# The 16 small products of y's u part in each RWKV unit queued behind the unit's last chain product (1 core, float32 decoder layer)

## The chip, the cores and the metric

The kernel runs on one core of a Trainium2 chip. Every time is a device time in microseconds (us) of that core. A version's time is the median of its runs; one further execution is recorded by the hardware profiler, and all rows and intervals in this text are from that execution. TensorE is called PE (its weight loads PEld), VectorE DVE, ScalarE ACT, GpSimd POOL, and SyncE, which issues most of the DMAs, SP.

## The reference

One decoder layer in float32, 1024 tokens by 1024 channels: a SwiGLU feed-forward (inner width 2816) with layer norm; a token mixer; layer norm; a second feed-forward with layer norm. The mixer projects the tokens through `w_in` and runs two branches side by side, an mLSTM (4 heads of 256, chunks of 128 tokens) and an RWKV-7 recurrence (16 heads of 64), multiplies each branch with its weights, gates them with sigmoids, adds them and multiplies with `w_out`. The RWKV recurrence is

```python
def step(st, xs):
    r_t, w_t, k_t, v_t, a_t, b_t = xs
    sa = jnp.einsum('bhvk,bhk->bhv', st, a_t)
    st = st * w_t[:, :, None, :] + sa[..., None] * b_t[:, :, None, :] + v_t[..., None] * k_t[:, :, None, :]
    return st, jnp.einsum('bhvk,bhk->bhv', st, r_t)
```

The change touches how the outputs y of that recurrence are put together. No arithmetic is added or removed.

## The kernel before

**Stages.** Phase A is the first feed-forward, B the `w_in` projections and the RWKV recurrence, C the mLSTM with the branch product of RWKV, D the rest of the mixer and the second feed-forward. The large products are made as three products of split operands (L128, L129, L130; moving tile 128x512 or 128x256, type float32r). Those of phase B that nothing nearby waits for are called fillers here: `fillers` traces them with the lowest priority, and the scheduler puts them wherever PE would have nothing else. Their result goes to a `psg` tile. The RWKV projections for the next head pair go to `psa` by the same three lines.

**RWKV units.** A unit `u` is one pair of heads (`p = u // 2`) and one half of the tokens (`hh = u % 2`), 8 chunks of 64 tokens. The 16 units are worked one after the other. `rwkv_half` prepares a unit, `rwkv_scores` makes its score tiles `SC` (L495), `rwkv_inverse` fills the V part of the tile `UV` (transposes L551, ACT copies L554, POOL memsets L555) and inverts the triangular parts (L573, L580). `rwkv_post` normalises y and stores it to `yrD`.

**The chain.** `rwkv_chain` is serial over the 8 chunks of a unit: L599 and L600 add up the right-hand side in `psc`, DVE copies it into `RW` (L601, a view of the tile `AR`), L603 multiplies it by the inverse into `psd`, DVE copies that product, called u, into the free half of chunk n's `UV` (L605), L609 makes the state update, POOL decays the old state (L612) and DVE adds the two (L614); then the next chunk's L600 needs the new state. L603 is the unit's last chain product for chunk 7.

**y's u part.** `rwkv_out` makes 16 products `SC` by u of 64x64x64 in float32 (L629) into one `psb` tile: the even chunks (e = 0) first, a DVE addition (L630), then the odd chunks, and a second addition. A float32 matmul is issued once in the program and stands as two passes in the trace, so the 16 are the 32 of the change's name. Each product needs only its own chunk's u.

**What sets the order.** Each engine works through its own queue in order. That queue is laid down when the program is built: a scheduler takes traced instructions by priority as they become ready in its own reckoning. Chain and `rwkv_out` are both traced at priority 3000, inverse at 2000, fillers lowest. `psb` and `UV` have two buffers each, used in turn.

Of the kernel before, what the change touches and what calls it, by code (L numbers as in the profile page):

```python
# [30 lines left out]
class Net:  # L31
# [551 lines left out]
    def rwkv_chain(self, o):  # L583
        nc = self.nc
        AR, SC, BN, UV, XT, PC = (o[k] for k in ("AR", "SC", "BN", "UV", "XT", "PC"))
        H = [slice(0, 64), slice(64, 128)]
        fl = lambda t: t.rearrange("p h v -> p (h v)")

        RW = AR.rearrange("p n (e c) -> p (n e) c", c=P)
        if o["hh"] == 0:  # L590
            for h in range(2):
                nc.gpsimd.memset(self.Sbuf[1][H[h], h], 0.0)
        S = self.Sbuf[1]
        for n in range(8):
            n2, e = n // 2, n % 2
            bs = H[1 - e]
            pc = self.ps("c", (P, 2, 64))
            for h in range(2):
                nc.tensor.matmul(pc[:, h], SC[:, e, n2, h], UV[:, n, H[h]], start=h == 0, stop=False)  # L599
            nc.tensor.matmul(fl(pc), AR[:, n2, e * P:(e + 1) * P], fl(S), start=False, stop=True)  # L600
            nc.vector.tensor_copy(RW[:, n], fl(pc))  # L601
            pu = self.ps("d", (P, 2, 64))
            nc.tensor.matmul(fl(pu), fl(XT[:, e, n2]), RW[:, n], start=True, stop=True)  # L603
            for h in range(2):
                nc.vector.tensor_copy(UV[bs, n, H[h]], pu[H[h], h])  # L605
            if o["hh"] == 1 and n == 7:
                break
            pS = self.ps("d", (P, 2, 64))
            nc.tensor.matmul(fl(pS), BN[:, n], UV[:, n], start=True, stop=True)  # L609
            S1 = self.Sbuf[n % 2]  # L610
            pcn = PC[:, n:n + 1]
            nc.gpsimd.tensor_scalar(S1, S, pcn, None, op0=ALU.mult)  # L612
            for h in range(2):
                nc.vector.scalar_tensor_tensor(S1[H[h], h], pS[H[h], h], pcn[H[h]], S1[H[h], h],  # L614
                                               op0=ALU.mult, op1=ALU.add)
            S = S1
# [412 lines left out]
def build(tc, ins, out):  # L1029
    with ExitStack() as ctx:  # L1030
        net = Net(ctx, tc, ins, out)
        nc = tc.nc
# [26 lines left out]
        with net.phase("B", VB=4):  # L1059
            net.rwkv_small(x1T)  # L1060
            with net.low():
                for f in net.fillers(x1T):
                    f()
            pr = net.rwkv_prep(x1T, 0)
            units = [net.rwkv_half(pr, 0)]
            net.mlstm_gates(x1T)
            units.append(net.rwkv_half(pr, 1))
            net.rwkv_scores(units[0])
            net.rwkv_inverse(units[0])
            net.rwkv_scores(units[1])  # L1070
            for u in range(16):
                if u % 2 == 0 and u < 14:
                    pr = net.rwkv_prep(x1T, u // 2 + 1)
                with net.high(3000):
                    net.rwkv_chain(units[u])
                    net.rwkv_out(units[u])
                if u % 2 and u < 14:
                    units.append(net.rwkv_half(pr, 1))
                if u < 15:
                    with net.high(2000):  # L1080
                        net.rwkv_inverse(units[u + 1])
                if u % 2 == 0 and u < 14:
                    units.append(net.rwkv_half(pr, 0))
                if u < 14:
                    with net.high(3000):
                        net.rwkv_scores(units[u + 2])
                net.rwkv_post(units[u])
# [83 lines left out]
```

## Time and profile before

| | us |
|---|---|
| median of 3 runs (3355.88 to 3357.31) | 3355.94 |
| the profiled execution | 3345.49 |
| its span, first to last instruction | 3343.8 |
| PE busy | 3183.2 (95%) |
| DVE busy | 1706.0 (51%) |
| ACT busy | 832.3 (25%) |
| POOL busy | 760.9 (23%) |

The profiled execution took 3345.49 us, 0.31% less than the median. Its span leaves 1.7 us outside. PE is busy in nearly every slice, so what a step costs is read best from the starts of matmuls that follow each other: the durations of neighbouring matmuls overlap.

### The profile page before, as it was taken

The page shows a single profiled execution, that of the slowest core. Times are in us where ns is not written, and L with a number is a line of the kernel's source. Part 1 is how long each engine was busy: PE and PEld are TensorE (multiplying, and loading weights), DVE is VectorE, ACT ScalarE, POOL GpSimd, SP SyncE. Part 2 cuts the span into 40 slices and gives each one's busy share as a digit, 9 for nine tenths or more (in the row PEclk, how much of TensorE's full clock was granted, in tenths as well). Part 3 has the DMA queues.
Part 4 walks back from the last instruction along what each step waited for, and adds up shares of the span by engine and source line. Part 5 has one row for each costly group of instructions (what it writes and reads, how often), then busy time and mean ns, then how long its engine had stood idle before and what let it go on. Part 6 is the DMA issues. An engine that isn't in the chain of part 4 may idle for free. (4 is left out here: it accounts for less than half of the span.)

```text
span 3343.8 us, 43277 instructions
## 1 busy us (share of the span) xinstructions
PE 3183.2 (95%) x16344; PEld 2585.9 (77%) x16344; DVE 1706.0 (51%) x4350; ACT 832.3 (25%) x1327; POOL 760.9 (23%) x755
## 2 busy tenths in 40 slices
PE   9999999998899999999999999999988999999997
PEld 7888888877677777887877777777776888888886
DVE  3323222264647676757667675576478322232227
ACT  3121112122312231313222221464333211111111
POOL 3222222222212222222222131200003222222212
PEclk9999999999989999999999999999999999999999
DMA  4111111113222232222232333554562111111111
GB/s 152 51 44 44 51 51 51 45 45 88 59 57 65 66 85 64 73 58 70 68 75 58 79 85 82 184 183 140 182 222 92 57 51 46 50 44 57 45 32 51
DMA packets 386903, 259.33 MB, mean 78 GB/s; under 512 B 102365, under 2 KB 342151, under 8 KB 386695
## 3 DMA queue, kind: packets, MB, share of 16 engines
q1 hardware_dynamic: 379783, 243.98, 25.1%
q0 software_dynamic: 4608, 8.39, 0.9%
q10 hardware_dynamic: 2304, 4.20, 0.3%
q8 instruction: 129, 2.11, 0.3%
q14 instruction: 79, 0.65, 0.1%
HBM read 203.02 MB, written 53.48 MB: 77 GB/s over the span
## 5 line engine op out<-in xcount | busy, mean ns | idle before, releaser
L206 DVE SCALAR_TENSOR_TENSOR v<-v,psb 128x512 f32<-128x512 f32 (+1 forms) x92 | 61.1, 665 | 737.3 <-PE psb L130 726.6
L232 DVE SCALAR_TENSOR_TENSOR u<-u,psc 128x512 f32<-128x512 f32 x416 | 282.8, 685 | 209.6 <-PE psc L130 205.6
L128 PE MATMUL psc<-u,u 128*128 128x512 f32 x832 | 331.1, 398 | 15.5 <-DVE u L232 7.0
L128 PE MATMUL psg<-xT,w 128*128 128x512 f32 (+1 forms) x856 | 329.9, 385 | 8.6 <-DVE v L962 6.0
L129 PE MATMUL psg<-xT,w 128*128 128x512 f32 (+1 forms) x856 | 330.3, 386 | 0.6 <-DVE xT L112 0.6
L129 PE MATMUL psc<-u,u 128*128 128x512 f32 x832 | 326.7, 393 | 3.4 <-DVE u L112 3.4
L130 PE MATMUL psg<-xT,w 128*128 128x512 f32 (+1 forms) x856 | 328.9, 384 | 0.0
L130 PE MATMUL psc<-u,u 128*128 128x512 f32 x832 | 326.7, 393 | 2.1 <-DVE u L112 2.0
L128 PE MATMUL psg<-xT,wf 128*128 128x512 f32 x776 | 316.9, 408 | 4.4 <-DVE f L686 2.1
L112 POOL TENSOR_TENSOR wf<-rawf,wf 128x512 fp32r<-128x512 f32 x186 | 255.4, 1393 | 280.3 <-ACT wf L108 243.0
L129 PE MATMUL psg<-xT,wf 128*128 128x512 f32 x776 | 317.2, 409 | 0.0
L130 PE MATMUL psg<-xT,wf 128*128 128x512 f32 x776 | 317.1, 409 | 0.0
L112 POOL TENSOR_TENSOR w<-raw,w 128x512 fp32r<-128x512 f32 x139 | 176.9, 1292 | 581.2 <-ACT w L108 513.9
L130 PE MATMUL psb<-xT,wf 128*128 128x512 f32 (+1 forms) x744 | 284.7, 383 | 0.0
L128 PE MATMUL psb<-xT,wf 128*128 128x512 f32 (+1 forms) x744 | 284.1, 382 | 0.5 <-ACT wf L108 0.5
L129 PE MATMUL psb<-xT,wf 128*128 128x512 f32 (+1 forms) x744 | 284.3, 382 | 0.0
L112 POOL TENSOR_TENSOR u<-u,u 128x1024 fp32r<-128x1024 f32 x44 | 105.5, 2398 | 603.3 <-ACT u L108 425.0
L108 ACT CAST w<-raw 128x512 fp32r<-128x512 f32 x163 | 96.8, 616 | 477.7 <-PE psg L129 176.0
L128 PEld LDWEIGHTS psc<-u,u 128*128 128x128 f32 x832 | 157.5, 189 | 63.6 <-DVE u L232 21.3
L108 ACT CAST wf<-rawf 128x512 fp32r<-128x512 f32 x210 | 123.4, 619 | 332.1 <-PE psg L129 154.8
L128 PEld LDWEIGHTS psg<-xT,w 128*128 128x128 f32 x856 | 161.4, 189 | 42.9 <-DVE v L962 6.8
L129 PEld LDWEIGHTS psg<-xT,w 128*128 128x128 f32 x856 | 161.4, 189 | 32.8 <-DVE xT L112 2.1
(325 smaller groups left out, 6108.4 us busy)
## 6 DMA issues: line engine op xcount, KB each, us to landing
rawf<-in_w_in_dram SPq DMA_DIRECT2D x98, 256.0 KB
raw<-in_ffn_w_gate_dram SPq DMA_DIRECT2D x88, 256.0 KB
rawf<-in_ffn_w_up_dram SPq DMA_DIRECT2D x88, 256.0 KB
u<-in_ffn_w_down_dram SPq DMA_DIRECT2D x44, 512.0 KB
raw<-in_w_in_dram SPq DMA_DIRECT2D x50, 256.0 KB
qkD<-f SPq DMA_DIRECT2D x32, 256.0 KB
v<-wadD POOLq DMA_DIRECT2D x32, 256.0 KB, 4.0
gD<-f SPq DMA_DIRECT2D x32, 256.0 KB
```

The source lines that it names most:

```text
L108: nc.scalar.copy(hi, src)
L112: eng.tensor_tensor(lo, src, hi.bitcast(F32), op=ALU.subtract)
L128: mm(out, a[0], b[0], start=first, stop=False)
L129: mm(out, a[0], b[1], start=False, stop=False)
L130: mm(out, a[1], b[0], start=False, stop=last)
L206: nc.vector.scalar_tensor_tensor(hf, sg, 0.5, pu, op0=ALU.mult, op1=ALU.mult)
L232: nc.vector.scalar_tensor_tensor(yd, yd, ALPHA if first else 1.0, po, op0=ALU.mult, op1=ALU.add)
```

## The change

The last L603 of a unit is kept (`o["last"]`, overwritten in each chunk), and `rwkv_out` is traced inside `tc.issue_after` of it. That adds an edge of order, and no wait for completion, from each PE instruction of `rwkv_out` to that product: on PE no L629 of a unit may stand ahead of the unit's last L603. Other engines get no edge.

```diff
@@ rwkv_chain
             pu = self.ps("d", (P, 2, 64))
-            nc.tensor.matmul(fl(pu), fl(XT[:, e, n2]), RW[:, n], start=True, stop=True)
+            o["last"] = nc.tensor.matmul(fl(pu), fl(XT[:, e, n2]), RW[:, n], start=True, stop=True)
@@ build
                     net.rwkv_chain(units[u])
-                    net.rwkv_out(units[u])
+                    with tc.issue_after(units[u]["last"].ins):
+                        net.rwkv_out(units[u])
```

The scheduler lays all later queues anew, so the order differs from unit 0 until the end of phase C. Counted over the whole of PE's queue, the 256 L629 stand in 99 rows of the order before (a row is a run of like instructions with nothing between) and in 46 after. In units with odd number they stood as 8 and 8 already; in the even ones and in unit 15 they stood in up to 11 places. The other small products stand in nearly the same number of rows: L599 128 before and 132 after, L495 41 and 42, L551 17 and 18, L660 23 and 24, L437 21 and 20, all others unchanged.

PE's queue in the middle of unit 2's chain before: L603 with one chunk's u product, L609 with its state update, L629 with y's products of unit 2, L130, L128 and L129 with fillers, L599 already of unit 3.

```order
L603 MATMUL psd_11281<-AR_10303,XT_735_5121 128x128
L599 MATMUL psc_11623<-UV_11323,SC_10804 128x64 x2
L130 MATMUL psg_6022<-xT_4577,wf_6013 128x512
L629 MATMUL psb_11304<-UV_10749,SC_10378 64x64
L128 MATMUL psg_6022<-xT_4577,wf_6012 128x512
L609 MATMUL psd_11285<-UV_10749,BN_10488 128x128
L629 MATMUL psb_11304<-UV_10749,SC_10378 64x64
L129 MATMUL psg_6022<-xT_4578,wf_6012 128x512
```

Here two of y's products stand alone, one between fillers and one behind the state update. The same unit's end after, from its last L603 (L551 are the V transposes of unit 3, into whose `UV` the L599 of unit 3 look):

```order
L603 MATMUL psd_11295<-AR_10303,XT_735_5121 128x128
L629 MATMUL psb_11304<-UV_10749,SC_10378 64x64 x7
L609 MATMUL psd_11299<-UV_10749,BN_10488 128x128
L629 MATMUL psb_11304<-UV_10749,SC_10378 64x64
L551 MATMUL psb_11324<-ident,vv_10111 128x128 x4
L130 MATMUL psg_6098<-xT_4577,wf_6089 128x512
L128 MATMUL psg_6126<-xT_4881,wf_6088 128x512
L129 MATMUL psg_6126<-xT_4882,wf_6088 128x512
L130 MATMUL psg_6126<-xT_4881,wf_6089 128x512
L599 MATMUL psc_11623<-UV_11323,SC_10804 128x64 x2
L600 MATMUL psc_11623<-S_734_5118,AR_10674 128x128
```

The even chunks' products stand together behind the last chain product, and unit 3's L551, which stood some 100 rows ahead of unit 2's last L629 before, and its first L599, which stood 25 rows ahead of it, stand behind them; the odd chunks' products follow.

PE's queue in phase C, at the second mLSTM chunk (L886, L892, L896, L905 are mLSTM products; `psg_8902` is a `w_in` filler, `psg_18532` the first tile of RWKV's branch product, which reads the tiles `xT_17846` and `xT_17847` made from the stored y), before:

```order
L129 MATMUL psg_8902<-xT_4578,wf_8892 128x512
L130 MATMUL psg_8902<-xT_4577,wf_8893 128x512
L905 MATMUL psa_18096<-v_2723_18042,kw_18072 128x257
L886 MATMUL psb_18080<-ident,kT_18037 128x128 x4
L892 MATMUL psc_18088<-v_2723_18042,v_18056 128x257
```

and after:

```order
L129 MATMUL psg_18532<-xT_17847,w_18512 128x512
L130 MATMUL psg_18532<-xT_17846,w_18513 128x512
L905 MATMUL psa_18096<-v_2723_18042,kw_18072 128x257
L886 MATMUL psb_18080<-ident,kT_18037 128x128 x4
L892 MATMUL psc_18088<-v_2723_18042,v_18056 128x257
```

At the same place of the mLSTM the `w_in` fillers are used up, and the branch product stands there. Before, it began in the fourth mLSTM chunk. In all, unit 15's last L629 has 7072 of the large products ahead of it instead of 6997.

## Rows read from the trace of the kernel before

**Rows 1.** Busy time of two stretches: the RWKV units, and phase C. Columns: stretch, its length, busy us of PE, PEld, DVE, ACT and POOL with the number of instructions, granted TensorE clock, DMA share, GB/s.

```profile
958.00:2123.00 1165.00, 1103.62 (x6925) 889.40 (x6926) 771.74 (x2684) 285.13 (x467) 278.41 (x403) 0.96 0.27 69
2123.00:2386.00 263.00, 252.10 (x1220) 200.25 (x1219) 164.91 (x441) 145.95 (x224) 23.41 (x24) 1.00 0.62 191
```

**Rows 2.** Waits of PE between 958 and 2123 us, longest first: who waited for whom, us in total, times, longest one.

```profile
PE psb L479 <- ACT v L108: 22.1, 7, 4.8
PE psb L573 <- DVE X L565: 7.8, 6, 5.2
```

**Rows 3.** The timeline of PE in unit 2's chain: start, us, engine, line, operation, output and inputs, tile of the array, moving tile, count.

```profile
1157.63 0.38 PE L609 MATMUL psd<-UV,BN 128*128 128x128 f32 x2
1157.77 0.48 PE L129 MATMUL psg<-xT,wf 128*128 128x512 f32 x1
1158.08 0.40 PE L130 MATMUL psg<-xT,wf 128*128 128x512 f32 x1
1158.32 0.39 PE L128 MATMUL psg<-xT,wf 128*128 128x512 f32 x1
...
1160.83 0.47 PE L130 MATMUL psg<-xT,wf 128*128 128x512 f32 x1
1161.24 0.33 PE L629 MATMUL psb<-UV,SC 64*64 64x64 f32 x2
1161.49 0.50 PE L128 MATMUL psg<-xT,wf 128*128 128x512 f32 x1
1161.83 0.38 PE L609 MATMUL psd<-UV,BN 128*128 128x128 f32 x2
1162.14 0.33 PE L629 MATMUL psb<-UV,SC 64*64 64x64 f32 x2
1162.40 0.50 PE L129 MATMUL psg<-xT,wf 128*128 128x512 f32 x1
1162.73 0.39 PE L130 MATMUL psg<-xT,wf 128*128 128x512 f32 x1
...
1164.20 0.91 PE L629 MATMUL psb<-UV,SC 64*64 64x64 f32 x12
1165.04 0.50 PE L129 MATMUL psg<-xT,wf 128*128 128x512 f32 x1
```

**Rows 4.** The timeline of PE at y's products of unit 3, an odd unit.

```profile
1228.92 1.14 PE L629 MATMUL psb<-UV,SC 64*64 64x64 f32 x16
1230.00 0.50 PE L130 MATMUL psa<-xT,w 128*128 128x512 f32 x1
```

**Rows 5.** Busy time and clock of the stretch around those rows, columns as in rows 1.

```profile
1224.00:1231.00 7.00, 7.00 (x56) 5.31 (x56) 3.57 (x10) 0.64 (x2) 1.14 (x2) 1.00 0.73 184
```

**Rows 6.** Line 629 as a whole: who waited for it (us, times).

```profile
  POOL UV L555: 21.7, 5
  DVE AR L630: 13.8, 15
```

**Rows 7.** Line 554, ACT's copies of the transposed V into `UV`: durations, and who waited for it (us, times).

```profile
L554 ACT COPY UV<-psb x32: 579/581/584, 920.1 to 2046.3; 64x512 f32<-64x512 f32 x32
...
  PEld psc L599: 0.4, 2
```

**Rows 8.** Busy time and clock of two stretches with little PE work, and of the stretch behind each; columns as in rows 1.

```profile
1468.00:1473.80 5.80, 2.24 (x16) 1.87 (x16) 5.80 (x27) 1.90 (x3) 2.53 (x2) 1.00 0.30 67
1473.80:1477.20 3.40, 3.40 (x18) 3.40 (x17) 2.92 (x14) 0.00 (x0) 0.00 (x0) 0.50 0.38 126
1555.00:1559.10 4.10, 1.36 (x11) 1.16 (x10) 4.10 (x8) 0.95 (x2) 2.76 (x4) 1.00 0.50 116
1559.10:1562.50 3.40, 3.40 (x14) 3.04 (x14) 2.40 (x7) 1.89 (x3) 0.00 (x0) 0.50 0.34 117
```

**Rows 9.** Waits of all engines between 2219 and 2240 us, where RWKV's branch product begins, columns as in rows 2.

```profile
ACT xT L108 <- DMA rT<-yrD: 2.8, 4, 1.5
PEld psg L129 <- DVE xT L112: 2.1, 5, 1.1
PEld psg L128 <- ACT xT L108: 2.0, 4, 1.0
...
PE psg L129 <- DVE xT L112: 0.6, 1, 0.6
...
PE psg L128 <- ACT xT L108: 0.5, 1, 0.5
```

**Rows 10.** Busy time and DMA of the second mLSTM chunk's surroundings and of the place of rows 9; columns as in rows 1.

```profile
2140.00:2170.00 30.00, 28.55 (x156) 23.79 (x155) 18.26 (x53) 24.69 (x34) 6.42 (x5) 1.00 1.00 303
2220.00:2240.00 20.00, 18.43 (x81) 12.83 (x80) 18.27 (x49) 12.29 (x19) 0.11 (x1) 1.00 0.86 282
```

**Rows 11.** The instructions on the tile `rT`, through which the stored y comes back: durations min/median/max in ns, first and last start, forms. L108 is ACT's high part, L112 DVE's low part, L944 the load of y.

```profile
L108 ACT CAST xT<-rT x24: 607/619/1052, 2202.8 to 2376.0; 128x512 fp32r<-128x512 f32 x16, 128x1024 fp32r<-128x1024 f32 x8
L112 DVE TENSOR_TENSOR xT<-rT,xT x24: 679/692/1226, 2204.1 to 2377.4; 128x512 fp32r<-128x512 f32 x16, 128x1024 fp32r<-128x1024 f32 x8
L944 SPq DMA_DIRECT2D rT<-yrD x8: 319/332/462, 2132.3 to 2228.7; - x8
```

## The prediction

> **What bounds the kernel now.** I read the busy time by stretch first. In the stretch of the RWKV units PE is busy 1103.6 of 1165 us; DVE, next, has 771.7 [rows 1]. Fillers close most holes of the chain, so this stretch ends when PE has issued its products, and its price is that of PE's queue: products, the steps between unlike ones, waits, and time at the lower clock. The list of waits says what is left open: 22.1 us in 7 waits of L479 for an ACT cast of its operand, 7.8 us for L573 [rows 2]; none of the long ones is for y's products. [...]
>
> The timeline of PE shows what y's products cost there, by start to start. Two fillers of which the first stands behind a float32 product take 0.55 us (1157.77 to 1158.32); with a single product of y (two passes) between such two, 1160.83 to 1161.83, 1.00 us: the product costs 0.45 us. From L609 over one filler to the next start it is 0.45 us (1157.63 to 1158.08), and with a product of y behind L609 0.90 us (1161.83 to 1162.73): again 0.45 us [rows 3]. In a run 12 passes take 0.84 us to the next start (1164.20 to 1165.04) [rows 3], and 16 take 1.08 us [rows 4]: four more passes for 0.24 us, so a product inside a run costs 0.12 us. Most of the price of a lone product lies in the steps into and out of it.
>
> **The change part by part.** *Steps removed.* The order has the L629 in 99 places before and 46 after, so 53 are gone. Each saves 0.45 less 0.12, 0.33 us: 53 x 0.33 = 17.5 us, all on PE and on the path while fillers remain. Fillers do remain: unit 15's end moves 75 large products later, and `w_in` fillers still stand behind it.
>
> *Steps added.* Other small products stand in 6 more places (L599 4, L495, L551 and L660 1 each, L437 one fewer). At the same 0.33 us this gives back 2.0 us. Net: 15.5 us.
>
> [...] The rows show a lone product paying about 0.1 us on its way in and 0.1 on its way out, and a filler behind L609, a product of full tile size, paying its 0.08 too (0.31 against 0.23). [...]
>
> *What waits for the moved products.* DVE's two additions per unit, L630, waited for them 13.8 us in 15 waits, and POOL's memset L555 of the next unit's `UV` 21.7 us in 5 [rows 6]. Behind L630 on DVE stand chain copies (L601, L605); a run of 16 passes holds them at most 1.08 us [rows 4], and in the units with odd number it does so already. Behind L555 on POOL stand the decays L612 of the next chain; the new order puts the first of them ahead of the memset. I take nothing for either; without the fillers' cover it would be a microsecond per unit.
>
> *V part of the next unit.* The transposes L551 of an odd unit now stand between the runs of the unit before, four fillers ahead of its first L599, where they had tens of products' time. Between them ACT must copy, twice 0.58 us. The even units already have that short distance, and PE's loads waited there 0.4 us in all [rows 7]. Bounds for the other 8 units: nothing, to one uncovered copy each, 4.6 us. I take 0.4 us, the row for the same step.
>
> *Start of phase C.* By unit 15's end 75 more large products are used up, so the branch product of RWKV comes in the second mLSTM chunk instead of the fourth. It needs y back through `rT`: 8 loads, 16 ACT casts of 0.62 us and 16 DVE subtractions of 0.69 us [rows 11]. At its old place PE and its loads waited 5.2 us for them (2.1 + 2.0 + 0.6 + 0.5) [rows 9]. The new place is fuller: the DMA engines' share is 1.00 against 0.86 there, ACT is busy 24.7 of 30 us against 12.3 of 20 [rows 10]. Bounds: the 5.2 us vanish, or all 8 loads lie open. At 303 GB/s [rows 10] 8 x 0.52 MB take 13.9 us, with the last cast pair and subtraction about 16. I take half as much again as now, 2.6 us more, because ACT's share there is about a third higher and the loads are the same.
>
> *The rest.* The chain's own links keep three to four fillers between them before and after, and phases A and D keep their order. Nothing is taken for them.
>
> Sum: -17.5 + 2.0 + 0.4 + 2.6 = -12.5 us. The profiled execution would go from 3345.49 to 3333.0 us. The median stands 10.45 us above that execution; with the same difference the forecast is 3355.94 - 12.5 = 3343.4 us, rounded 3343.
>
> **The rivals.** *New waits eat it.* The whole queue of the stretch is laid anew, and PE's long waits (L479, L573) are meetings of queues that nobody arranged. Such a wait costs twice. From 1555.0 to 1559.1 PE was busy 1.36 of 4.10 us, then the granted clock stood at 0.50 for 3.4 us; the same after 1468 [rows 8]. That is 2.7 us lost and half of 3.4: 4.4 us. Three more of them than now take 13.2 us: about 3356, no change. For it: 7 such waits at one place already. Against: the distance from a unit's sigmoids to its L479 in PE's order is nearly as before, and waits can vanish as well.
>
> *The branch product stalls phase C.* If the start in the second chunk comes before the y rows are back, PE's queue stands with the mLSTM's products behind it. With the 16 us of loads, casts and subtractions all open, four of the mLSTM's own loads of the same size between them (4 x 1.7 us at the same rate, 6.9 us), and half of 3.4 us at the lower clock, this is about 24 us; less 15.5 it is +8.5: 3364, slower. It decides from 22 us lost there (15.5 + 6.7). For it: rows 9 and 10. Against: stores of the first six y rows end long before, and three loads can run ahead.
>
> *The run is too thin for the clock.* Behind thin stretches the clock has fallen [rows 8]. [...] By the rows, half of 3.4 us in each of the 9 units whose products are gathered would be 15.3 us, and with it the time would stay at 3356. Against it stands an odd unit: with both runs in it, the stretch 1224 to 1231 us had a clock of 1.00 [rows 5].
>
> *More than forecast.* The new queue may lose waits instead of gaining them: with three fewer of the 4.4 us kind 3343 becomes 3330.
>
> *It does not do what it says.* The order shows that it does, but in the odd units there was nothing to gather, and the two runs of a unit stay apart because of the addition between them. That is in the count of 46.
>
> **How the numbers follow.** About 0.2%, 6.7 us, is what a measurement can tell from no change: faster is below 3349.2, slower above 3362.7. The forecast has a chance of 0.56; its own spread is 3336 to 3351, and 0.05 of it lies within 0.2%. New waits have 0.20 (0.16 no change, 0.04 slower), the stall in phase C 0.12, the clock 0.04, more than forecast 0.08. Faster: 0.51 + 0.08 = 0.59; same: 0.05 + 0.16 + 0.04 = 0.25; slower: 0.04 + 0.12 = 0.16. For the range I leave out the outer part of the stall's case and the best of the good one: 3327, all 17.5 us saved, the 5.2 us gone and one and a half long waits fewer, up to 3362.
>
> **What would show it.** In the profile after, L629 should have about as many passes as now, in long runs, and lone pairs between fillers only rarely. PE's busy time in the RWKV stretch should fall by more than ten microseconds, for the same products. Waits of PE for `UV` copies (L554) should stay below a microsecond in sum, and the waits for `xT` at the start of the branch product below some 8 us. The forecast is wrong if a lone product's 0.45 us turns up elsewhere, if the list of waits grows by three or more long ones, or if phase C holds a gap in PE's timeline at its second chunk.

## The result, and the profile after

| | before | after | ratio, 95% interval |
|---|---|---|---|
| first timing, medians of 4 and 4 executions, us | 3356.62 | 3325.06 (3318.87 to 3333.11) | 0.9917, 0.9895 to 0.9938 |
| again, of the run after_again below, 11 and 4 | 3355.22 | 3318.47 (3312.94 to 3319.47) | 0.9890, 0.9869 to 0.9910 |
| profiled executions, us | 3345.49 | 3333.11, again 3319.47 | |

The change is faster, by 31.6 and 36.8 us between medians; 12.5 were forecast. The forecast of 3343 had the sign but far too little of the gain; the time lies 2 us below the range's lower end of 3327.

Executions of one kernel differ by 15 to 20 us, mostly with their mean granted clock (after: 3312.94 us at 0.980 to 3333.11 at 0.973; before: 3343.15 at 0.975 to 3362.00 at 0.971); the first profile of after (clock 0.973) is its slowest execution, while that of before (0.975) is one of its faster ones. So the profiled fall of 12.4 us equals the forecast by luck. The second profile of after had 0.978.

The same two stretches as in [rows 1], of after:

```profile
958.00:2123.00 1165.00, 1105.53 (x6943) 894.43 (x6944) 770.06 (x2662) 288.14 (x471) 275.81 (x406) 0.95 0.27 71
2123.00:2386.00 263.00, 252.85 (x1236) 201.39 (x1235) 172.92 (x470) 155.13 (x231) 19.08 (x20) 0.99 0.63 196
```

PE's busy time in a stretch hardly shows what was saved: the stretch is a fixed time that PE fills either way, and more instructions fit in (6943 against 6925). The timeline shows it. At the end of unit 2 (compare [rows 3]) no product of y is left between the fillers. But at the chain link L609, which had one behind and one ahead of it, PE now waits for u:

```profile
1159.13 0.39 PE L128 MATMUL psg<-xT,wf 128*128 128x512 f32 x1
1160.89 0.46 PE L609 MATMUL psd<-UV,BN 128*128 128x128 f32 x2 [1.37 <-DVE UV L605]
...
1164.65 0.49 PE L603 MATMUL psd<-AR,XT 128*128 128x128 f32 x2
1165.07 1.02 PE L629 MATMUL psb<-UV,SC 64*64 64x64 f32 x14
1166.03 0.49 PE L609 MATMUL psd<-UV,BN 128*128 128x128 f32 x2
1166.45 0.33 PE L629 MATMUL psb<-UV,SC 64*64 64x64 f32 x2
...
1170.13 0.91 PE L629 MATMUL psb<-UV,SC 64*64 64x64 f32 x12
1170.97 0.50 PE L128 MATMUL psg<-xT,wf 128*128 128x512 f32 x1
```

The timeline of DVE ahead of that wait shows why u came late. L603 had started at 1157.90. The two copies of u (L605) stand in DVE's queue behind instructions of the next unit's inverse (L528, L530) and of the mLSTM's convolution (L686):

```profile
1157.72 1.01 DVE L528 TENSOR_TENSOR fs<-L,X 128x72 f32<-128x72 f32 x1
1158.65 0.74 DVE L686 SCALAR_TENSOR_TENSOR f<-psg,vt,f 128x511 f32<-128x511 f32 x1
1159.31 0.67 DVE L530 TENSOR_TENSOR X<-X,fs 128x72 f32<-128x72 f32 x1
1160.01 0.22 DVE L605 COPY UV<-psd 64x64 f32<-64x64 f32 x1
...
1160.51 0.23 DVE L605 COPY UV<-psd 64x64 f32<-64x64 f32 x1
```

PE's waits in the same stretch, to set beside [rows 2]: L479 waits 5.7 us less, L573 2.2 more, and two links of the chain have come up (at L609 the list names L530, which ran on DVE beside the copies of u).

```profile
PE psb L479 <- ACT v L108: 16.4, 7, 4.3
PE psb L573 <- DVE X L565: 10.0, 7, 4.9
PE psd L603 <- DVE AR L601: 6.1, 9, 1.6
PE psd L609 <- DVE X L530: 4.7, 4, 1.7
```

The idle time of PE and its loads, added up, ahead of a line, and until when (us, times): L609 after, L603 after, and y's L629 before. Ahead of L609 it is 25.5 us in all, with two smaller rows, where before it was 7.1; ahead of L603 32.1 with a row of 7.2, where it was 22.1. Ahead of L629 before it was 20.8, the first of ten rows being the wait for the same copy of u; after it is 9.3, and none of it for u. Most of this is idle time of the loads, in which PE can be at work: PE's own is 15.5 of the 57.6 us ahead of the two links after (8.3 at L609, 7.2 at L603), where it was 5.4 of 29.2, and at L629 it was 0.3 and is nothing.

```profile
  issue: 10.8, 14
  DVE X L530: 4.7, 4
  PE psg L130: 4.5, 7
  DVE UV L605: 2.7, 3
```

```profile
  DVE AR L601: 24.9, 50
```

```profile
  DVE UV L605: 6.7, 22
```

The lines that answer to [rows 6] and [rows 7], of L629 and of L554 after: DVE's addition waits 10 us more for y's products, POOL 2 us more, and PE's loads 1.8 us for the copies of the V part.

```profile
  POOL UV L555: 24.0, 7
  DVE AR L630: 23.9, 24
```

```profile
  PEld psc L599: 1.8, 9
```

The branch product begins in the second mLSTM chunk. Its waits there, between 2150 and 2200 us (compare [rows 9]):

```profile
PEld psg L128 <- ACT xT L108: 3.1, 3, 2.7
ACT xT L108 <- DMA rT<-yrD: 3.0, 1, 3.0
PE psg L128 <- ACT xT L108: 2.3, 1, 2.3
...
PEld psg L129 <- DVE xT L112: 0.4, 2, 0.2
```

That is 5.8 us for PE and its loads, where 5.2 was the old sum and 7.8 the forecast. Elsewhere in phase C PE waits less: for L892 it waited 4.1 us before and 0.5 after, between 2123 and 2386 us.

```profile
PE psc L892 <- ACT ti L898: 4.1, 5, 1.1
```

```profile
PE psc L892 <- ACT ti L898: 0.5, 1, 0.5
```

**An account of PE's queue.** For every trace I took the interval from each matmul's start to the next and compared it with the median interval of the same three neighbouring kinds of matmul at full clock, over all the traces (a kind is a line with its shapes; L128, L129 and L130 count as one line). The sum of these medians is *steps*, the products with the steps between them; what is longer is *waits*, and at a granted clock of 0.50 up to twice the median is *lower clock*. A line that waits nearly always has some of its wait in the median, so a difference between two kernels is better than a sum. The line between steps and waits depends on how the kinds are drawn: by shape alone, with the three lines apart, or with the tiles' names, the same traces give 11 to 22 us less steps from before to after and 14 less to no fewer waits, while the two together fall by 21 to 25 us each time. First to last matmul, us, one execution each:

| kernel | places of L629 | steps | waits | lower clock | sum |
|---|---|---|---|---|---|
| before | 99 | 3106.8 | 156.4 | 61.3 | 3324.5 |
| after, first profile | 46 | 3090.6 | 150.2 | 71.2 | 3312.2 |
| after, second profile | 46 | 3090.6 | 149.2 | 58.7 | 3298.5 |
| relaid_only | 98 | 3110.0 | 152.8 | 72.9 | 3335.7 |
| first_half | 80 | 3101.2 | 147.9 | 60.2 | 3309.3 |
| second_half | 68 | 3098.0 | 163.7 | 67.0 | 3328.7 |
| one_run | 24 | 3080.1 | 153.6 | 63.5 | 3297.2 |
| both_products_first | 85 | 3104.0 | 143.6 | 56.8 | 3304.3 |
| out_first | 91 | 3106.6 | 158.0 | 61.7 | 3326.3 |

The two profiles of after agree to 1 us in steps and waits and differ by 12.5 us in the lower clock. A mean over executions can do without the account: span times (1 - clock) is my estimate of what the lower level cost at most, work at 0.50 taken as twice as long (two passes took 0.43 us instead of 0.22 in the run called steps below; the account finds three quarters to four fifths of it: 61.3 of 83.6 us in the profile of before, 71.2 of 89.9 and 58.7 of 73.0 in those of after). Over the 49 executions of before in the experiments it has a mean of 88.0 us, over the 8 of after 77.2; but the four of after's first timing have 83.1 and the four of the second 71.3. The rest of the span, 3263.8 and 3242.5 us, falls by 21.3.

### The profile page after: what moved, and what is told of

Its sections match the earlier page's. It is cut to its first block, busy times and chain, and to the rows that moved or that the text cites. A ratio compares the mean times of both kernels' runs of the same rounds, so it can differ in the third digit from the quotient of the medians.

```text
span 3331.4 us, 43285 instructions
## 1 busy us (share of the span) xinstructions
PE 3178.7 (95%) x16344; PEld 2586.6 (78%) x16344; DVE 1705.8 (51%) x4350; ACT 841.7 (25%) x1334; POOL 752.9 (23%) x755
## 5 line engine op out<-in xcount | busy, mean ns | idle before, releaser
L128 PE MATMUL psc<-u,u 128*128 128x512 f32 x832 | 331.3, 398 | 14.7 <-DVE u L232 6.7
L128 PE MATMUL psg<-xT,w 128*128 128x512 f32 (+1 forms) x856 | 331.4, 387 | 11.7 <-DVE v L962 7.5
L129 PE MATMUL psg<-xT,w 128*128 128x512 f32 (+1 forms) x856 | 331.3, 387 | 0.0
L129 PE MATMUL psc<-u,u 128*128 128x512 f32 x832 | 327.2, 393 | 3.4 <-DVE u L112 3.4
L130 PE MATMUL psg<-xT,w 128*128 128x512 f32 (+1 forms) x856 | 329.9, 385 | 0.0
L130 PE MATMUL psc<-u,u 128*128 128x512 f32 x832 | 327.3, 394 | 2.1 <-DVE u L112 2.0
L128 PE MATMUL psg<-xT,wf 128*128 128x512 f32 x776 | 318.3, 410 | 0.7 <-ACT f L698 0.7
L130 PE MATMUL psg<-xT,wf 128*128 128x512 f32 x776 | 318.9, 411 | 0.0
L112 POOL TENSOR_TENSOR wf<-rawf,wf 128x512 fp32r<-128x512 f32 x186 | 251.2, 1370 | 295.3 <-ACT wf L108 255.6
L129 PE MATMUL psg<-xT,wf 128*128 128x512 f32 x776 | 317.1, 409 | 0.0
L112 POOL TENSOR_TENSOR w<-raw,w 128x512 fp32r<-128x512 f32 x139 | 176.9, 1291 | 587.0 <-ACT w L108 509.7
L130 PE MATMUL psb<-xT,wf 128*128 128x512 f32 (+1 forms) x744 | 284.2, 382 | 0.0
L128 PE MATMUL psb<-xT,wf 128*128 128x512 f32 (+1 forms) x744 | 283.6, 381 | 0.5 <-ACT wf L108 0.5
L129 PE MATMUL psb<-xT,wf 128*128 128x512 f32 (+1 forms) x744 | 283.9, 382 | 0.0
L112 POOL TENSOR_TENSOR u<-u,u 128x1024 fp32r<-128x1024 f32 x44 | 105.4, 2396 | 603.1 <-ACT u L108 428.4
L108 ACT CAST w<-raw 128x512 fp32r<-128x512 f32 x163 | 96.3, 616 | 480.5 <-PE psg L129 178.5
L128 PEld LDWEIGHTS psc<-u,u 128*128 128x128 f32 x832 | 157.5, 189 | 61.9 <-DVE u L232 20.2
L108 ACT CAST wf<-rawf 128x512 fp32r<-128x512 f32 x210 | 123.1, 619 | 322.1 <-issue 149.2
L128 PEld LDWEIGHTS psg<-xT,w 128*128 128x128 f32 x856 | 162.0, 189 | 44.9 <-DVE v L962 8.4
L130 PEld LDWEIGHTS psc<-u,u 128*128 128x128 f32 x832 | 157.8, 190 | 37.9 <-DVE u L112 3.3
```

The costliest lines, as they stand in the source:

```text
L108: nc.scalar.copy(hi, src)
L112: eng.tensor_tensor(lo, src, hi.bitcast(F32), op=ALU.subtract)
L128: mm(out, a[0], b[0], start=first, stop=False)
L129: mm(out, a[0], b[1], start=False, stop=False)
L130: mm(out, a[1], b[0], start=False, stop=last)
```

## The experiments

Theory at the start: the 53 places gone are worth 0.33 us each, and the rest of the 31.6 us is what a new laying of the queue draws in waits and lower clock. Rivals: a place is worth more than 0.33 us; or the first timing was lucky in its clock. Medians with the number of executions; the kernel before ran on the same chip in each group.

### relaid_only: the queue laid anew, the places kept

```diff
-                with net.high(3000):
+                with net.high(3200):
                     net.rwkv_chain(units[u])
+                with net.high(3000):
                     net.rwkv_out(units[u])
```

> The chain is traced at priority 3200 instead of 3000 and y's products stay at 3000: the whole queue is laid anew, but y's products still stand in 98 places of PE's queue (99 before). 14 more places of other small products (L495 8, L540 3, L551 4, L660 4 fewer, and so on). Steps theory (each lone place costs 0.33 us, nothing else matters): 98 places are 0.3 us less, 11 to 14 others 4 us more, so +1 to +6 us against before. Re-laying theory (the fall comes from waits and lower-clock time that are drawn anew with any new order): any value, a fall of 10 us or more is possible without one place gone.

3361.59 us (12) against 3354.53 (23): 1.0024, 1.0013 to 1.0035. With 98 places instead of 99, the time rises by 7 us. In the account steps rise by 3.2, waits fall by 3.6 and the lower clock costs 11.6 more; the clock of its 12 executions lay between 0.969 and 0.972, that of the 23 of before between 0.971 and 0.976. A new order alone moves the time, and this one for the worse.

### first_half and second_half: the edge for half of the units

```diff
-                    with tc.issue_after(units[u]["last"].ins):
+                    with tc.issue_after(units[u]["last"].ins) if u < 8 else ExitStack():
```

> The edge of order only for units 0 to 7: 80 places instead of 99 (46 in the full change). Steps theory: 19 places x 0.33 = 6.3 us less than before, with 4 other places more about 5 us less. If the fall of the full change (31 us in the medians) were all proportional to places, 31 / 53 x 19 = 11 us less. Re-laying theory: no relation to the number of places.

> The edge of order only for units 8 to 15: 68 places instead of 99. Steps theory: 31 x 0.33 = 10.2 us less than before. Proportional to the medians' fall: 31 / 53 x 31 = 18 us less. Re-laying theory: no relation to the number of places.

(`u >= 8` in second_half.) first_half, 80 places: 3329.92 us (6), 0.9935, 0.9918 to 0.9952. second_half, 68 places: 3342.01 us (12), 0.9970, 0.9957 to 0.9982. The half with fewer places gone (19 against 31) gained twice as much, 24.6 us against 12.5. So the gain doesn't follow the places. The steps do: 5.6 us for 19 and 8.8 for 31, 0.29 and 0.28 us each. Nor does it hang on L479 alone: in first_half, PE waited 20.8 us for it, where it was 22.1 before.

### one_run: the products of a unit in one run

The changed kernel, with all 16 products traced ahead of the two additions. The second loop header stands ahead of the addition, the first loop ends with the products.

```diff
             for n2 in range(4):
                 for h in range(2):
                     nc.tensor.matmul(py[ks, n2, h], SC[bs, e, n2, h, ks], UV[bs, 2 * n2 + e, H[h]], start=True, stop=True)
+        for e in range(2):
+            ks = H[e]
             nc.vector.tensor_tensor(Y[ks], py[ks], AR[ks, :, e * P:e * P + P].rearrange("p n (h v) -> p n h v", v=64),
                                     op=ALU.add)
```

> The full change, and in addition all 16 products of a unit are traced before the two DVE additions, so that they stand in 24 places instead of 46. Steps theory: 22 x 0.33 = 7.3 us less than the changed kernel, 22 to 25 us less than before by steps alone (75 places). Proportional to the medians' fall: 13 us less than the changed kernel. Re-laying theory: no relation; may also be slower than the changed kernel. A wait that grows: DVE's first addition comes 1 us later, so a few tenths per unit more before the next unit's copies.

3318.10 us (5), 0.9892, 0.9875 to 0.9909. Another 22 places fewer than after take another 10.5 us of steps away, 0.48 each. But the time is that of after (3319.5 is the median of its 8 executions): the waits for a DMA at L447, 3.1 us in the trace of after, stand at the head of the list, and the account has 4 us more of waits.

```profile
PE psb L447 <- DMA v<-wadD: 14.3, 8, 2.6
PE psb L479 <- ACT v L108: 12.7, 5, 4.0
```

### steps: what makes a lone product dear

A kernel without the layer (its output is zeros). Fillers of the kernel's form are broken by one float32 product after every four, 24 times, and then 24 such products follow in a run; so for a 64x64 product, for one of full tile size with 64 columns, and for one of 64x128.

```diff
+        for _ in range(24):
+            small()
+            fill(4)
+        for _ in range(24):
+            small()
+        fill(96)
```

> Leaves out the whole layer and writes zeros: only fillers (split product of 128x512) and small float32 products stand on PE, nothing waits. Three sections, each of 24 times one small product and four fillers, then 24 small products as a run: tile 64x64, tile 128x128 with 64 columns moving, tile 64x128. Steps theory: a period of four fillers and one lone 64x64 product takes 4 x 0.227 + 0.45 = 1.36 us, a product in the run 0.12 us. If only a change of the tile's mode costs, the lone full-size product takes about 0.22 us of its own (its passes alone, as in the run) and its period 1.13 us or less; if any float32 product between fillers costs the step, its period is 1.3 us or more and the loss per lone product is like that of the 64x64 one.

PE's timeline, the end of each section (start, us, engine, line, tile of the array, moving tile, count of passes): L1047 are the fillers, L1050 the 64x64 products, L1053 the full ones, L1056 those of 64x128.

```profile
58.10 0.33 PE L1050 MATMUL px<-raw 64*64 64x64 f32 x2
58.36 1.19 PE L1047 MATMUL pf<-big,wt 128*128 128x512 f32 x4
59.48 3.01 PE L1050 MATMUL px<-raw 64*64 64x64 f32 x48
62.42 22.10 PE L1047 MATMUL pf<-big,wt 128*128 128x512 f32 x96
84.36 0.33 PE L1053 MATMUL px<-raw 128*128 128x64 f32 x2
...
110.83 0.33 PE L1053 MATMUL px<-raw 128*128 128x64 f32 x2
...
111.98 5.46 PE L1053 MATMUL px<-raw 128*128 128x64 f32 x48
117.25 22.05 PE L1047 MATMUL pf<-big,wt 128*128 128x512 f32 x96
...
173.48 0.43 PE L1056 MATMUL px<-raw 64*128 64x64 f32 x2
...
174.97 6.96 PE L1056 MATMUL px<-raw 64*128 64x64 f32 x48
```

A filler takes (84.36 - 62.42) / 96 = 0.2285 us, four 0.91. A lone 64x64 product adds 59.48 - 58.10 - 0.91 = 0.47 us, in a run it takes 2.94 / 24 = 0.12: 0.34 is saved by gathering. A full-size one adds 111.98 - 110.83 - 0.91 = 0.24 alone and takes 5.27 / 24 = 0.22 in a run: 0.02 is saved. One of 64x128 adds 0.58 alone. Its run can't be divided like that, for the clock fell inside it (columns: stretch, length, PE, PEld, DVE, POOL, clock, DMA share, GB/s):

```profile
174.97:178.88 3.91, 3.91 (x36) 3.91 (x36) 0.00 (x0) 0.00 (x0) 1.00 0.02 4
178.88:185.71 6.83, 6.83 (x24) 5.94 (x24) 0.00 (x0) 0.00 (x0) 0.50 0.00 0
```

At full clock two of its passes take 0.22 us from start to start, so 0.36 is saved; at the lower clock they take 0.43. So in this run the price of being alone came with another tile of the array (0.34 and 0.36 us against 0.02), not with float32 between float32r products. PE was busy all the time in the 3.91 us of such products after which the granted clock fell to 0.50; it did not fall in the run of 64x64 products (2.94 us) or in that of full-size ones (5.27 us). This is one execution, and no run varies the length.

### both_products_first: the trace order alone, without the edge

The kernel before with one_run's two lines.

> Without the edge of order, but with all 16 products traced before the two additions: 85 places instead of 99. Steps theory, at the 0.34 to 0.37 us per place that the profiles of the first four kernels give: 5 us less by steps. With waits and lower-clock time drawn anew, the time as a whole -12 to +6 us against before. If the additional gain of the kernel with 24 places came from the order of the additions and not from the places gone, this kernel would show most of it: 7 us or more beside the steps.

3324.44 us (4) against 3353.08 (15): 0.9915, 0.9902 to 0.9929. This was not expected: 14 places fewer, 2.8 us less of steps, and as fast as the change. The sign set down for the order of the additions, 7 us or more beside the steps, is met nearly four times over; whether it is that order or any other laying of the queue, this run can't tell. The waits of its trace between 958 and 2123 us:

```profile
PE psb L447 <- DMA v<-wadD: 16.4, 8, 3.0
PE psb L573 <- DVE X L565: 8.5, 4, 5.1
PE psc L600 <- DVE S L614: 5.1, 8, 1.3
PE psb L479 <- ACT v L108: 5.0, 3, 4.0
```

L479 waits 17.1 us less than in [rows 2], L447 11.7 more. In the account waits fall by 12.8 and the lower clock by 4.5; over its executions, by span times (1 - clock), the lower clock cost at most 73.1 us instead of 88.0.

### out_first: y's products ahead of the chain

```diff
                 with net.high(3000):
                     net.rwkv_chain(units[u])
+                with net.high(3500):
                     net.rwkv_out(units[u])
```

> Y's products traced at priority 3500, above the chain's 3000, no edge: 91 places instead of 99, another queue laid anew. Steps theory: 8 x 0.35 = 3 us less by steps; the sum of steps read from the profile between 3105 and 3112 us against 3111 before. The time as a whole within 3340 to 3365 us, since waits and lower-clock time are drawn anew.

3350.95 us (11), 0.9991, 0.9981 to 1.0001, 91 places: no difference. Its clock lay between 0.974 and 0.979, above every execution of relaid_only, with nearly the same products and places. So the level of a kernel's clock differs between orders of the queue, but not by the order alone: the four executions of after's first timing lay at 0.973 to 0.976, the four of its second at 0.977 to 0.980. And a higher clock does not by itself bring time: here the lower clock cost up to 8.9 us less, and the rest of the span grew by 5.9.

### before_nosum and after_nosum: the line with the longest waits taken out

In both, the sums over each head (L479, L480) and the cast and subtraction ahead of them are left out.

```diff
-        hi, lo = (self.s("v", [P, 512], F32R, bufs=self.VB) for _ in range(2))
-        self.split(t1, hi, lo, lo_eng="dve")
-        pq = self.ps("b")
-        nc.tensor.matmul(pq, self.same, hi, start=True, stop=False)
-        nc.tensor.matmul(pq, self.same, lo, start=False, stop=True)
         bv = self.half(tag="bv")
-        nc.vector.tensor_tensor(bv, pq, o["V"][hh], op=ALU.mult)
+        nc.vector.tensor_tensor(bv, t1, o["V"][hh], op=ALU.mult)
```

> The kernel before, with the sums over each head (L479 and L480, 32 large products) and the cast and subtraction ahead of them left out; bv is then the product of the unsummed row and V, so this part of the output is not the reference's. Its order has y's u part in 100 places, about as before. Theory (a wait of L479 costs its own length and a stretch at the lower clock behind it, and nothing else takes its place): 32 x 0.23 = 7.3 us of products, 22.1 us of waits and half of about 3.4 us behind each of 7, 11.9 us: 41 us less, about 0.988; at least 29 us less if the clock does not come back. Rival (PE only waits for the next late operand instead): 7 to 12 us less, 0.996 to 0.998.

> The changed kernel with the same part left out as in before_nosum; its order has y's u part in 39 places, 61 fewer than there. Theory (the places are worth 0.33 us each, and what the change gave beyond that came from waits of L479 and the clock behind them): 61 x 0.33 = 20 us below before_nosum. Rival (each new laying of the queue draws its own waits, at other lines as well): the steps still fall by 20 us, but the distance of the two times can lie anywhere from 0 to 40 us, and the difference from 20 must then show as waits or lower clock at other lines than L479.

before_nosum: 3322.41 us (6) against 3355.22 (11), 0.9901, 0.9883 to 0.9919. after_nosum: 3303.86 us (4), 0.9850, 0.9825 to 0.9874. Taking the line out of before gives 32.8 us, of which its products are 7.3 by their count. Its waits were not saved: others have come up in their place, as the list of before_nosum between 958 and 2123 us shows (`pj` L334 at 4.7 us before). All of PE's listed waits there are 60.0 us, where they were 61.7 with L479's 22.1 among them.

```profile
PE psa L128 <- DVE pj L334: 15.4, 9, 4.2
PE psb L490 <- DVE SC L494: 9.2, 12, 2.7
PE psb L447 <- DMA v<-wadD: 9.2, 6, 2.5
```

Between the two kernels without the line, 61 places make 18.5 us between medians, where 20 were expected (steps in the account: 20.1). With the line in both, the same change makes 31.6 to 36.8. That looks like the theory that the surplus hangs on L479's waits, but the parts speak for the rival: in the account waits rise by 8 us from before_nosum to after_nosum and the lower clock costs 5 less, so the time came near the steps by luck. L479's list of waits also fell by only 5.7 us from before to after.

### after_again: the change, executed again

> The changed kernel once more, in more rounds. If the 31.6 us between the medians of the first timing are the change's own, the ratio lies at 0.989 to 0.992 again. If the clock of those few executions was the cause and steps and waits alone are the change's, the ratio is 0.994 to 0.996.

0.9890 (table at the top). The first timing was no luck of a few executions: the surplus over the steps comes again with this order of the queue, though with a higher clock than in the first timing. The second profile of after has the same waits as the first (L479 16.7 us in 7, L603 6.1 in 9).

## Why the prediction came out as it did

**Steps removed: held.** 17.5 less 2.0 us were forecast, 16.2 measured in the account (11 to 22 with the kinds drawn otherwise); the micro-kernel's 0.34 us for 53 places makes 18.0. A place gone is worth 0.28 to 0.36 us in the five comparisons with 19 to 75 places against a kernel without the edge. The 22 of one_run against after give 0.48, and in the three with 14 or fewer (2.8 us for 14, 0.2 for 8, 3.2 more for 1), where other small products move about as much, the count says little. In the run called steps only the products on another tile pay for being alone, 0.34 us for 64x64 and 0.36 for 64x128, where a full-size one pays 0.02. The way in and the way out of a lone product, read as about 0.1 us each, measure 0.34 together there. The filler's 0.08 behind L609 is no such price: in steps the four fillers behind a lone full-size product take 1.01 us (110.97 to 111.98) instead of 0.91, and it still costs hardly more alone, 0.24 us, than the 0.22 in a run.

**New waits of DVE, POOL and PEld: nearly as forecast.** DVE and POOL wait 12 us more for y; nothing was taken for that, and no wait of PE at L603 or L609 follows one of L630's. L554's copies made 1.8 us of waits of PE's loads where 0.4 were taken, within the bounds of 0 to 4.6 but above the one microsecond set down as a sign.

**The chain's links: costed wrongly.** "Nothing is taken for them", because three to four fillers stay between the links. They do stay, but PE's own idle time ahead of L609 and L603 rose by 10.1 us. It would be natural to put this down to y's products, which no longer cover the wait for u. The trace does not bear that out. PE waits at eight L609 after, and two to five large products stand between L603 and each, about as much work as at the same links before. Only one of the eight, that of the timeline above, had a product of y there before. What changed is the copy of u: at these eight it ends 1.6 to 3.2 us after the start of L603, where before it ended after 0.9 to 1.4. At most of them DVE has L528, L530 (up to 1.3 us) or L686 ahead of it. The waits at L603 are alike: the copy L601 comes later, and no product of y had stood there. The new laying changed DVE's queue too, and the sum had looked there only at L630.

**New waits eat it, and more than forecast: both happened.** L479's meeting of queues, which nobody arranged, lost 5.7 us in the list of waits; the account has 10 to 11 less waits there, but 5 more in the medians. In the RWKV stretch the account's waits stayed where they were, 61.0 us before, 61.5 and 60.3 after: the links' new waits and the lost ones cancel.

**Start of phase C: too dear.** 2.6 us more were forecast; the branch product's waits are 5.8 us against 5.2, and in all of phase C waits fall by 4 to 5 us, because L892's and those of the last unit (L660, 2.1 us) are gone. So the waits of the whole kernel, forecast 3.0 us higher, are 6 to 7 us lower in the account.

**The clock: not priced.** The rival that a thin run would drop it is not seen here: in neither profile of after was a run of y's products at the lower clock, or did the clock fall in the 7 us behind one. These runs last 1.1 us at most; that longer ones are safe isn't shown, as the fall inside the 64x128 run of steps says. But that the clock would be the same was a term too, put at nothing. By the executions' means the lower level costs up to 10.8 us less in after, about 8 by the account's share, and the two timings differ by as much. With steps -16.2, waits -6 to -7 and this, the sum is -30 to -34 us; the means of all executions lie 32.1 apart. The likeliest case added -15.5, +3.0 and 0: the steps were right, and the waits and the clock were each off by about 10.

**What stays open.** Why after's order gives a higher mean clock than before's, and why its two timings differ. Shorter long waits are one candidate (both_products_first has the fewest of L479 and a high clock), but one_run's clock (0.976 to 0.977) is no higher than after's, and I changed the order and the waits together each time. So about half of the measured gain is counted, as waits and clock, but its cause is not shown. A hold of L479 alone behind a later product was not tried. One sum of the prediction was slightly off, and nothing hangs on it: 8 x 0.52 MB at 303 GB/s take 13.7 us, not 13.9.

## What to carry to other kernels

Gathering small products that use another tile of the array was worth 0.28 to 0.36 us here, about a third of a microsecond, for each place where PE changes over and back (0.34 in steps), and the places can be counted from the order. Where the whole queue is laid anew by it, allow for waits and clock as well: here orders with about the same products lay 7 us above and 29 us below the first one, so a trial of several orders can be worth as much as the change. And when a link of a chain begins to wait, look at the engine that makes its operand before blaming what moved on the waiting one: here DVE had other work ahead of the copies.

## What the runs showed of the hardware that was not expected

The lower clock was not a fixed answer to the program here. Two executions of after at the same place of the same queue (1270.0 to 1280.8 and 1280.8 to 1294.5 us, columns as in rows 1), the first profile and then the second:

```profile
1270.00:1280.80 10.80, 9.01 (x74) 6.82 (x73) 2.27 (x6) 1.06 (x2) 0.00 (x0) 1.00 0.40 96
1280.80:1294.50 13.70, 13.70 (x77) 11.57 (x75) 3.78 (x8) 2.81 (x6) 1.26 (x6) 0.50 0.04 7
```

```profile
1270.00:1280.80 10.80, 9.37 (x80) 6.98 (x79) 1.78 (x5) 1.78 (x4) 0.00 (x0) 1.00 0.38 93
1280.80:1294.50 13.70, 13.47 (x100) 10.90 (x100) 7.13 (x18) 2.67 (x5) 4.48 (x9) 1.00 0.31 73
```

PE was busy 9.01 and 9.37 of 10.80 us; the rest is one wait of L573, of 1.8 and 1.4 us. Behind that stretch the granted clock stood at 0.50, the lower of the two levels in these rows, for 13.7 us in the one and not at all in the other: 77 matmuls instead of 100. Nor did a busy PE always keep the clock up: in steps it fell to 0.50 after 3.91 us of 64x128 products with PE busy all the time.
